# Expert weights stored in DRAM tile by tile, with one 4096-byte run a partition for each tile load

## The chip, the cores and the metric

One core of a Trainium2 chip runs the whole program. The metric is the device time in microseconds (us) of one execution. The engines are TensorE (PE; its weight loads are PEld), VectorE (DVE), ScalarE (ACT), GpSimd (POOL) and SyncE (SP), which here issues nearly all loads; 16 DMA engines move the bytes.

## The reference, cut to what matters

The program computes a one-layer hybrid block on 528 tokens, and then two layers of a second block on 512 latent tokens (and, in its first layer, 256 context tokens as well). Each of the two layers ends in a mixture of 16 experts, in which every expert takes its own best tokens:

```python
def ec_moe(h, w_router, w_gate, w_up, w_down):
    cap = EC_CAPACITY * n_tok // N_EXPERTS            # 64 of 512 tokens, 32 of 256
    aff = jax.nn.softmax(jnp.einsum('bnd,de->bne', h, w_router), axis=-1)
    g, idx = lax.top_k(jnp.swapaxes(aff, 1, 2), cap)
    xs = jax.vmap(lambda hb, ib: hb[ib])(h, idx)
    hid = jax.nn.silu(jnp.einsum('becd,edf->becf', xs, w_gate)) * jnp.einsum('becd,edf->becf', xs, w_up)
    ye = jnp.einsum('becf,efd->becd', hid, w_down) * g[..., None]
    return jax.vmap(lambda yb, ib: jnp.zeros((n_tok, d)).at[ib.reshape(-1)].add(yb.reshape(-1, d)))(ye, idx)
```

The model width and the experts' hidden width are both 1024, and all is float32. So `w_gate`, `w_up` and `w_down` hold 2 layers x 16 experts x 1024 x 1024 numbers each. Every weight is used once in an execution.

## The kernel before

`host_layout` arranges the inputs before the launch. The three expert tensors pass through it as they are. `body` traces the program; a planner orders the instructions of each engine, but inside `experts_both` the order of PE is that of the code.

In a layer the experts go two at a time, as eight pairs (`p_`, experts `ea` and `eb`). A pair needs its gate and up weights for each half `n` of the 1024 hidden columns, and then its down weights. All come as tiles of 256 rows by 512 columns, as `[128, 2, 512]`: 128 partitions, and in each of them two rows of 512 numbers (2048 bytes), which lie 128 rows apart in the matrix. A tile is 512 KB; a pair takes 32 tiles for gate and up and 16 for down, and a layer takes 384. `wtile` takes the next slot from a ring (`wslot`) and issues the load on SP's queue. A slot is free again when PE has used its old tile. The ring has NE + 6 + NX slots: 8 + 6 = 14 in layer 0 (`full`), 13 + 6 + 7 = 26 in layer 1. So the loads run ahead of PE by up to that many tiles.

In layer 0 `up_parts` and `down_parts` treat latent and context tokens together: `col4` (L139) runs four products side by side on strips of 32 columns of PE. In layer 1, the loop at L2235 to L2267, there are latent tokens alone, and `mm` (L136) runs two products side by side, on strips of 64 columns. In its first pairs the gathering of the chosen tokens (`next(more)`) is interleaved. After each pair `down_last` (L2036) scales the result and scatters it to the tokens. The last pair's results go through the final normalization (`last_norm`) to the output.

Of the kernel before, what the change touches and what calls it, by code (L numbers as in the profile page):

```python
# [26 lines left out]
def host_constants():  # L27

    p = np.arange(128)[:, None]
    c = np.arange(128)[None, :]  # L30
    parts = {}
    parts["ident"] = (p == c).astype(np.float32)
    sel = np.zeros((128, 8), np.float32)
    for i in range(3):
        sel[32 * i + np.arange(8), np.arange(8)] = -1.0
    parts["sel"] = sel
    parts["selm"] = ((p % 32 == c[:, :2]) & (p % 32 < 2)).astype(np.float32)
    parts["fbias"] = np.concatenate([np.zeros((128, 400)), np.where(c <= p, 0.0, NEG)], axis=1).astype(np.float32)
    t = (p % 64)
    parts["blk"] = ((p // 64) == (c // 64)).astype(np.float32)  # L40
    s = np.arange(64)[None, :]
    parts["low"] = (s <= t).astype(np.float32)
    parts["up"] = (t <= s).astype(np.float32)
    parts["sup"] = (t < s).astype(np.float32)
    for m in (1, 2, 4, 8, 16, 32):
        same = (t // (2 * m)) == (s // (2 * m))
        if m == 1:
            parts["lv1"] = (same & ((t // m) % 2 == 1) & ((s // m) % 2 == 0)).astype(np.float32)
        parts["lt%d" % m] = (same & ((s // m) % 2 == 1) & ((t // m) % 2 == 0)).astype(np.float32)
    parts["id64"] = (s == t).astype(np.float32)  # L50
    rs = np.ones((128, 576), np.float32)
    rs[:, ::64] = 0.0
    parts["reset"] = rs
    two = {}
    wlo = np.where(c >= p, 0.0, NEG)
    zero = np.zeros((128, 256))
    two["wb"] = np.concatenate([zero, wlo, zero[:, :128], np.where(c <= p, 0.0, NEG), zero], axis=1).astype(np.float32)
    two["flip"] = (((p // 64) == (c // 64)) & (p % 64 == 63 - c % 64)).astype(np.float32)
    tk = np.arange(SEQ)
    inv = (np.float32(10000.0) ** (-np.arange(16, dtype=np.float32) / np.float32(16))).astype(np.float32)  # L60
    d = np.arange(128) % 64
    pos = np.where((d < 32)[:, None], (tk // 64)[None, :], (tk % 64)[None, :]).astype(np.float32)
    ang = (pos * inv[d % 16][:, None]).astype(np.float32)
    two["cos"] = np.cos(ang).astype(np.float32)
    two["sin"] = (np.where(d % 32 < 16, -1.0, 1.0)[:, None] * np.sin(ang)).astype(np.float32)
    qc = (np.arange(128) % 64)[:, None]
    st = np.clip(qc - 8, 0, 48)
    kc = np.arange(64)[None, :]
    two["nmask"] = np.where((kc >= st) & (kc < st + 16), 0.0, NEG).astype(np.float32)
    two["mean"] = np.full((128, 128), 1.0 / 256, np.float32)  # L70
    two["iota1"] = np.tile(np.arange(1, 65, dtype=np.float32)[None, :], (128, 1))
    two["tokens"] = np.tile(np.arange(SEQ, dtype=np.float32)[None, :], (128, 1))

    def pack(parts):
        offs, cols, o = {}, [], 0
        for k, v in parts.items():
            offs[k] = (o, v.shape[1])
            cols.append(v)
            o += v.shape[1]
        return offs, np.ascontiguousarray(np.concatenate(cols, axis=1))  # L80
    return pack(parts) + pack(two)
# [10 lines left out]
def host_layout(given):  # L92

    g = dict(given)

    def cols(a, rows):
        return a.reshape(rows, 128).T
    v = [cols(g.pop(n), r) for n, r in VECTORS]
    v.append(g.pop("ffn_conv").reshape(3, 44, 128).transpose(2, 0, 1).reshape(128, 132))
    v.append(np.pad(g.pop("fox_f_bias").reshape(8, 1), ((0, 120), (0, 0))))  # L100
    v += [cols(g["norm_mix_post"], 8), cols(g["norm_ffn_pre"], 8),
          g["meta_tokens"][META - 2:].reshape(2, 8, 128).transpose(2, 1, 0).reshape(128, 16)]
    v += [cols(g.pop("c_2"), 8), cols(g.pop("c_ctx_2"), 8)]
    b = g.pop("b_mod_2")
    v += [cols(b[l], 48) for l in range(2)]
    c2 = [(g.pop(n), r) for n, r in CONV2]
    v += [cols(a[l], r) for l in range(2) for a, r in c2]
    g["vec"] = np.concatenate(v, axis=1)
    m = [np.concatenate([g.pop("rwkv_w_up")[0], g.pop("rwkv_a_up")[0]], axis=0), g.pop("rwkv_g_up")[0]]
    gates = [g.pop("lru_gate_a_w")[0], g.pop("lru_gate_x_w")[0]]  # L110
    for i in range(2):
        for w in gates:
            m.append(np.concatenate([np.pad(w[2 * i], ((0, 0), (0, 64))), np.pad(w[2 * i + 1], ((0, 0), (64, 0)))], axis=0))
    g["mats"] = np.concatenate(m, axis=1)
    g["nat_pad"] = np.pad(g.pop("nat_bias_2").reshape(-1), (64, 64))
    g["con"], g["con2"] = host_constants()[1::2]
    return g


# [7 lines left out]
def body(tc, A, out):  # L127
    nc = tc.nc
    ctx = ExitStack()
    PE, DV, AC, PL, SY = nc.tensor, nc.vector, nc.scalar, nc.gpsimd, nc.sync  # L130
# [28 lines left out]
    def nm(s):  # L159
        _n[0] += 1  # L160
        return "%s_%d" % (s, _n[0])
# [881 lines left out]
    for i in range(22):  # L1043
        res = []
        for hf in range(2):
# [5 lines left out]
            t = cv.tile([128, 512], F32, name=nm("cv"), tag="cv%d" % hf)  # L1051
# [98 lines left out]
    def layer(l):  # L1150
# [93 lines left out]
        for b in range(2):  # L1244
# [6 lines left out]
            n = 768 if full else 512  # L1251
# [3 lines left out]
            t = up_.tile([128, HW_], F32, name=nm("hx"), tag="hx%d" % b)  # L1255
# [229 lines left out]
        for i in range(4):  # L1485
# [4 lines left out]
            for j in range(4):  # L1490
# [3 lines left out]
                for h in range(2):  # L1494
                    ps = gps()
                    if j < 3:
                        c0, segs = 512 - w, [(512 - w, 128 * a0, w), (512, 512, 256)]
                    else:
                        c0, segs = 256, [(256, 512, 256), (512, 128 * a0, w)]
# [97 lines left out]
        for c in range(2 if full else 1):  # L1597
            t = rt.tile([128, 8, 16], F32, name=nm("wrm"), tag="wrm%d" % c)
# [5 lines left out]
            t = rt.tile([128, 16], F32, name=nm("brow"), tag="brow%d" % c)  # L1604
# [336 lines left out]
        def wslot(dt=F32):  # L1941
            i_ = ewn[0] % (NE + 6 + NX)
            ewn[0] += 1
            if i_ >= NE + 6:
                return ex.tile([128, 2, 512], dt, name=nm("ew"), tag="ew")
            if i_ < NE:
                return EW.tile([128, 2, 512], dt, name=nm("ew"), tag="ew")
            return WPw.tile([128, 2, 512], dt, name=nm("ew"), tag=("wr", "wh", "wl")[(i_ - NE) // 2], bufs=2)

        def wtile(name, e, k0, c0):  # L1950
            t = wslot()
            a = A[name]
            off = a.offset + ((l * 16 + e) * 1024 + 128 * k0) * 1024 + c0
            SY.dma_start(t, bass.AP(tensor=a.tensor, offset=off, ap=[[1024, 128], [128 * 1024, 2], [1, 512]]))
            return t

        if full:
# [78 lines left out]
        def down_last(p_, ea, eb, hT_):  # L2036
# [17 lines left out]
            for n, c in enumerate(HC):  # L2054
                for kh in range(4):
                    ws = [wtile("w_down_2", e, 2 * kh, 512 * n) for e in (ea, eb)]
                    for k in range(2):
                        K = 2 * kh + k
                        for po_, w_ in zip((0, 64), ws):
                            mm(psy[po_:po_ + 64, c], hT_[:, K, po_:po_ + 64], w_[:, k, :], K == 0, K == 7)  # L2060
                rows = norm_rows() if end and n else None
                t = outputs(psy, c, p_, t)
                if end and n:
                    g_ = gps()
                    for b in range(2):
                        hold(g_[:, HC[b]], 2 + b, 1)
                for b in range(4):
                    ps = held[b, n] if end else aps()
                    for i, y_ in enumerate(t[1:]):
                        mm(ps, oh_[:, 128 * b:128 * b + 128], y_, i == 0 and not end, i == 1)  # L2070
                    if not end:
                        DV.tensor_tensor(R_[b][:, c], R_[b][:, c], ps, ALU.add)
                if end:
                    skewed([last_norm(b, n, held[b, n], rows) for b in range(4)])
# [230 lines left out]
```

## Time and profile before

| | |
|---|---|
| median of 3 runs (lowest, highest) | 2784.72 us (2783.59, 2790.5) |
| the profiled execution, whole | 2780.72 us |
| its span, first to last instruction | 2778.9 us |
| PE busy in the span | 2578.3 us (93%) |
| moved by DMA | 578.65 MB, mean 208 GB/s |
| expert tile loads (3 tensors x 256 x 512 KB) | 768 |

The profiled execution is 4.0 us under the median of the runs, of which 1.8 us lie outside the span in any case. Layer 0's expert loads are issued from 1207 us on and its expert products run from 1305 to 1885 us; layer 1's run from 2258 to 2757 us. "DMA" in a row is the mean busy share of the 16 DMA engines. It is summed from the packets' own times, which overlap a little, so it can exceed 1.

### The profile page before, as it was taken

To read this page: it belongs to the slowest core of one execution; us is meant where nothing else is said; L and a number is where in the kernel's file an instruction comes from. 1 tells how busy PE (TensorE), PEld (TensorE's weight loads), DVE (VectorE), ACT (ScalarE), POOL (GpSimd) and SP (SyncE) were. 2 spreads that over 40 slices of the span, in tenths; PEclk is the share of its full clock that TensorE was granted. 3 is DMA by queue.
4 is the path that set the end of the run, shared out by engine and by line. 5 is a ranking of instruction groups with operands and counts; after the bars stand their busy time and mean duration, and the time that the engine had idled before them with its cause. 6 is when DMAs were issued, how large, how long until landed. Compare 5 with 4: busy or idle time off the path is not lost.

```text
span 2778.9 us, 46409 instructions
## 1 busy us (share of the span) xinstructions
PE 2578.3 (93%) x19286; PEld 1664.6 (60%) x19286; DVE 1217.6 (44%) x2252; ACT 898.5 (32%) x1617; POOL 161.4 (6%) x286
## 2 busy tenths in 40 slices
PE   7999999999998999996999999997999879999996
PEld 7877868999876877674333333324877744333322
DVE  4436555555656967565112121216868521121112
ACT  4344534343224357633211111116358421111001
POOL 0001000000000001013000000002001110000000
PEclk9999999999999999997999999997999979999999
DMA  4211144555762421424999999991430559999997
GB/s 141 61 36 42 36 160 137 180 162 173 237 210 81 96 49 49 140 91 155 333 386 345 381 345 380 347 340 43 104 77 18 199 203 387 386 386 386 387 387 275
DMA packets 378707, 578.65 MB, mean 208 GB/s; under 512 B 54384, under 2 KB 144880, under 8 KB 378240
## 3 DMA queue, kind: packets, MB, share of 16 engines
q1 hardware_dynamic: 354016, 550.82, 57.2%
q0 software_dynamic: 4928, 13.18, 1.9%
q10 hardware_dynamic: 19552, 11.68, 1.6%
q8 instruction: 152, 2.49, 0.4%
q14 instruction: 59, 0.48, 0.1%
HBM read 560.85 MB, written 5.24 MB: 204 GB/s over the span
## 4 chain that ended last, share of the span: by engine, by line
PE 65%; DVE 10%; DMA 10%; issue 4%; ACT 4%; POOL 2%; DVEq 0%; SPq 0%; ACTq 0%; POOLq 0%
PE g L136 26%; PE a L136 15%; PE g L139 11%; PE a L139 7%; DMA ew<-in_w_up_dram 6%; PE M L136 2%; DVE cy L1270 2%; DMA ew<-in_w_down_dram 2%; PE a L1409 2%; POOL rv L222 1%; DVE p L1382 1%; DMA wm<-in_w_mod_dram 1%; DVE wl L275 1%; DMA ln_g<-in_ln_g_dram 0%; DMA k<-k 0%
## 5 line engine op out<-in xcount | busy, mean ns | idle before, releaser
L136 PE MATMUL g<-ew,xsel 128*64 128x512 f32 x1024 | 262.7, 599 | 5.9 <-DMA ew<-in_w_up_dram 5.9
L139 PE MATMUL g<-ew,xsel 128*32 128x512 f32 x2048 | 254.1, 594 | 0.4 <-ACT xsel L1793 0.2
L275 DVE TENSOR_TENSOR wl<-wr,wh 128x1024 fp32r<-128x1024 f32 x95 | 115.2, 1213 | 187.9 <-ACT wh L274 179.5
L136 PEld LDWEIGHTS g<-ew,xsel 128*64 128x64 f32 x1024 | 75.9, 136 | 152.8 <-issue 113.8
L274 ACT ACTIVATE wh<-wr 128x1024 fp32r<-128x1024 f32 x95 | 99.6, 1049 | 189.1 <-PE g L136 121.1
L139 PEld LDWEIGHTS g<-ew,xsel 128*32 128x32 f32 x2048 | 68.3, 110 | 146.6 <-issue 136.0
L136 PE MATMUL g<-h2h,wh 128*128 128x256 f32 x704 | 144.1, 286 | 0.1
L136 PE MATMUL g<-h2h,wl 128*128 128x256 f32 x704 | 141.7, 283 | 0.0
L136 PE MATMUL g<-h2l,wh 128*128 128x256 f32 x704 | 141.3, 282 | 0.0
L139 PE MATMUL a<-ew,xsel 128*32 128x512 f32 x1024 | 140.0, 592 | 0.0
L136 PE MATMUL g<-ew,hT 128*64 128x512 f32 x512 | 131.2, 598 | 7.7 <-DVE y L2031 5.9
L139 PE MATMUL g<-ew,hT 128*32 128x512 f32 x1024 | 127.6, 605 | 4.0 <-DMA ew<-in_w_down_dram 4.0
L222 POOL TENSOR_TENSOR rv<-ru,epsc 128x1 f32<-128x1 f32 (+3 forms) x63 | 55.2, 880 | 1176.8 <-DVE ru L220 764.2
L2256 DVE TENSOR_TENSOR hid<-sg,g 128x512 f32<-128x512 f32 x16 | 11.0, 687 | 243.7 <-ACT sg L2255 219.5
L136 PEld LDWEIGHTS g<-h2h,wh 128*128 128x128 f32 x704 | 109.3, 190 | 10.5 <-ACT wh L274 7.4
L136 PEld LDWEIGHTS g<-h2h,wl 128*128 128x128 f32 x704 | 109.1, 190 | 0.0
L136 PEld LDWEIGHTS g<-h2l,wh 128*128 128x128 f32 x704 | 108.5, 189 | 0.4 <-issue 0.4
L1389 ACT ACTIVATE p<-p,mx 128x768 f32<-128x768 f32 (+4 forms) x120 | 91.6, 764 | 42.2 <-DVE mx L1382 39.9
L1270 DVE SCALAR_TENSOR_TENSOR cy<-hx,cvc,cy 128x798 f32<-128x798 f32 (+1 forms) x120 | 103.5, 898 | 1.8
L2148 DVE TENSOR_TENSOR hid<-sg,g 128x512 f32<-128x512 f32 x16 | 11.0, 688 | 207.9 <-ACT sg L2147 207.9
L136 PEld LDWEIGHTS g<-ew,hT 128*64 128x64 f32 x512 | 38.3, 136 | 88.2 <-issue 60.3
L1370 ACT ACTIVATE pT<-a 128x512 f32<-128x512 f32 (+1 forms) x152 | 78.2, 538 | 35.6 <-PE a L1409 33.0
(660 smaller groups left out, 5329.8 us busy)
## 6 DMA issues: line engine op xcount, KB each, us to landing
ew<-in_w_gate_dram SPq DMA_DIRECT2D x256, 512.0 KB, 10.8
ew<-in_w_up_dram SPq DMA_DIRECT2D x256, 512.0 KB, 10.5
ew<-in_w_down_dram SPq DMA_DIRECT2D x256, 512.0 KB, 10.8
wm<-in_w_mod_dram SPq DMA_DIRECT2D x96, 512.0 KB, 4.8
wr<-in_ffn_up_dram SPq DMA_DIRECT2D x44, 512.0 KB, 5.1
wr<-in_w_in_dram SPq DMA_DIRECT2D x42, 512.0 KB, 4.1
wr<-in_ffn_down_dram SPq DMA_DIRECT2D x22, 512.0 KB, 5.1
wr<-in_w_out_dram SPq DMA_DIRECT2D x16, 512.0 KB, 3.8
```

Source lines behind the costliest of these rows:

```text
L136: return PE.matmul(o, l, r, start=start, stop=stop, skip_group_check=True)
L139: PE.matmul(o, l, r, start=start, stop=stop, skip_group_check=True, tile_position=(0, o.start_partition()))
L222: PL.tensor_tensor(v[:P], u[:P], epsc[:P, :w], ALU.pow)
L274: AC.activation(hi, raw, AF.Copy)
L275: DV.tensor_tensor(lo, raw, f(hi), ALU.subtract)
L1270: DV.scalar_tensor_tensor(cy[b], hx[b][:, i:i + N], cvw[l][:, 2 * i + b:2 * i + b + 1], cy[b], ALU.mult, ALU.add)
L1370: AC.activation(dst, src, AF.Copy)
L1382: DV.tensor_tensor_reduce(t[:, n:n + w], v, b, -1.0, m, ALU.add, ALU.min, m2)
L1389: AC.activation(t[:, :e], t[:, :e], AF.Exp, scale=-1.0, bias=m, accum_out=sm)
L1409: PE.transpose(ps[:, 128 * i:128 * i + 128], t[:, 128 * i:128 * i + 128], ident)
L2148: DV.tensor_tensor(hid[:, 512 * n:512 * n + 512], sg, psx[:, 512:1024], ALU.mult)
L2256: DV.tensor_tensor(hid[:, 512 * n:512 * n + 512], sg, psx[:, 512:1024], ALU.mult)
```

## The change

The host now permutes each expert tensor to [layer, expert, block of 256 rows, half of the columns, partition, row of two, 512]. A tile of `wtile` is then one contiguous 512 KB piece of DRAM, in which each partition's two rows stand one behind the other: 4096 bytes a partition. The tile in SBUF, the slots, the queue, the number of loads and all arithmetic are as before.

```diff
     g["con"], g["con2"] = host_constants()[1::2]
+    for n in ("w_gate_2", "w_up_2", "w_down_2"):
+
+        g[n] = g[n].reshape(2, 16, 4, 2, 128, 2, 512).transpose(0, 1, 2, 5, 4, 3, 6)
     return g
...
         def wtile(name, e, k0, c0):
             t = wslot()
-            a = A[name]
-            off = a.offset + ((l * 16 + e) * 1024 + 128 * k0) * 1024 + c0
-            SY.dma_start(t, bass.AP(tensor=a.tensor, offset=off, ap=[[1024, 128], [128 * 1024, 2], [1, 512]]))
+            SY.dma_start(t, A[name][l, e, k0 // 2, c0 // 512])
             return t
```

## Rows read from the trace of the kernel before

**Rows 1.** The page's 40 equal slices of the span (69.5 us each).
```profile
PE   7999999999998999996999999997999879999996
DMA  4211144555762421424999999991430559999997
GB/s 141 61 36 42 36 160 137 180 162 173 237 210 81 96 49 49 140 91 155 333 386 345 381 345 380 347 340 43 104 77 18 199 203 387 386 386 386 387 387 275
```

**Rows 2.** Stretches in layer 1's experts: length, busy time (instructions), PEclk, DMA share, GB/s.
```profile
2260.00:2270.00 10.00, 10.00 (x62) 5.54 (x60) 0.00 (x0) 2.09 (x4) 0.00 (x0) 1.00 0.79 268
2270.00:2280.00 10.00, 10.00 (x56) 4.49 (x54) 0.00 (x0) 2.37 (x4) 0.00 (x0) 1.00 1.00 363
2280.00:2290.00 10.00, 10.00 (x54) 4.35 (x52) 0.69 (x1) 1.93 (x4) 0.00 (x0) 1.00 1.02 363
2300.00:2735.00 435.00, 409.75 (x1742) 153.90 (x1741) 68.76 (x117) 40.51 (x71) 0.00 (x0) 1.00 1.05 386
```

**Rows 3.** The chain that ended last, layer 1's experts: start, us, what.
```profile
2403.82 14.73 PE g L136 x66
...
2463.53 14.73 PE g L136 x66
...
2720.95 11.17 DMA ew<-in_w_up_dram
...
2732.16 2.80 PE g L136 x10
```

**Rows 4.** Waits of PE from 2253 to 2510 us: total us, times, longest.
```profile
PE a L1814 <- DVE tk L1811: 14.4, 1, 14.4
```

**Rows 5.** Waits of PE from 2510 to 2757 us.
```profile
PE g L136 <- DMA ew<-in_w_up_dram: 5.9, 19, 0.8
```

**Rows 6.** SP's loads as layer 1's experts begin: start, us, what.
```profile
2219.74 2.34 SPq L1954 DMA_DIRECT2D ew<-in_w_gate_dram  x2
2260.98 0.88 SPq L1954 DMA_DIRECT2D ew<-in_w_up_dram  x2
```

**Rows 7.** Stretches in layer 0's experts, columns as in rows 2.
```profile
1700.00:1750.00 50.00, 49.75 (x468) 15.83 (x464) 4.80 (x7) 4.63 (x8) 0.00 (x0) 1.00 1.05 386
1333.00:1885.00 552.00, 542.75 (x4777) 186.37 (x4769) 96.88 (x141) 69.54 (x115) 0.00 (x0) 0.99 0.98 359
```

**Rows 8.** Waits of PE from 1333 to 1885 us: the longest.
```profile
PE g L139 <- DMA ew<-in_w_down_dram: 4.0, 1, 4.0
```

**Rows 9.** The chain that ended last, at that wait.
```profile
1872.38 4.77 DMA ew<-in_w_down_dram
```

**Rows 10.** DMA from 2350 to 2700 us: packets, then SP's queue as share of 16 engines.
```profile
DMA packets 70076, 135.28 MB, mean 387 GB/s; under 512 B 4123, under 2 KB 4123, under 8 KB 70060
...
q1 hardware_dynamic: 70060, 135.06, 104.5%
```

**Rows 11.** DMA over the whole span: packets, the two instruction queues.
```profile
DMA packets 378707, 578.65 MB, mean 208 GB/s; under 512 B 54384, under 2 KB 144880, under 8 KB 378240
...
q8 instruction: 152, 2.49, 0.4%
q14 instruction: 59, 0.48, 0.1%
```

**Rows 12.** DMA issues over the span: count, KB each, median us to landing.
```profile
ew<-in_w_up_dram SPq DMA_DIRECT2D x256, 512.0 KB, 10.5
...
con<-in_con_dram SPq DMA_DIRECT2D x2, 1056.0 KB, 7.2
x<-in_x_dram SPq DMA_DIRECT2D x4, 512.0 KB, 7.3
```

**Rows 13.** DMA packets from 8 to 10 us, 752 to 754 us and 1116 to 1120 us.
```profile
DMA packets 237, 0.85 MB, mean 424 GB/s; under 512 B 26, under 2 KB 31, under 8 KB 237
...
DMA packets 230, 0.82 MB, mean 411 GB/s; under 512 B 23, under 2 KB 23, under 8 KB 230
...
DMA packets 425, 1.55 MB, mean 387 GB/s; under 512 B 47, under 2 KB 47, under 8 KB 425
```

## The prediction

> **What bounds the kernel now.** I read the slices of the span first [rows 1]. PE is busy nearly everywhere, so its busy time says little; what sets the expert stages apart is the DMA row. There are two stretches at 9, one in each layer's experts, and in layer 1 it stands flat at 386 or 387 GB/s. A flat rate under changing work suggests a limit of the transfers themselves, so I looked at each stage for who waits for whom.
>
> Layer 1 first. From 2300 to 2735 us the DMA engines move 386 GB/s at a share of 1.05 [rows 2]. A tile of 524,288 bytes at 386.5 GB/s (135.28 MB in 350 us [rows 10]) costs 1.357 us. PE alone is faster: while its work is the bound, one pair takes 59.7 us (2463.53 less 2403.82, the same piece of two successive pairs [rows 3]), and 59.7 / 48 tiles is 1.244 us a tile. So each pair falls 5.4 us behind its own consumption, and the 26 slots that were filled beforehand pay for it. One sees them pay: up to 2510 us PE's waits name no DMA at all, and the longest, 14.4 us, is for the choosing of tokens, ahead of the products [rows 4]; after it, PE waits for up tiles, 19 times [rows 5]. At the end the chain hangs on a load that lands at 2732.1 us, and PE goes on from there [rows 3]. That landing is set by the DMA rate since the ring was last full, not by PE.
>
> Layer 0 is the other case. There the four products side by side keep PE at 468 instructions in 50 us, with 49.75 us busy [rows 7], and the stage takes 552 us for 384 tiles, 1.44 us a tile: slower than a transfer (1.357). In the whole stage PE waits for a load once, 4.0 us [rows 8], and that is a load issued late, when its slot came free at 1872.38; its 4.77 us are mostly the latency of a load with few others beside it [rows 9]. The DMA row of 386 there is prefetching, not a bound.
>
> **The change, part by part.** *The permutation* is done before the launch and moves no instruction on the chip: nothing. *SP's issue:* still 768 loads, waits and slots alike; SP is paced by slots and landings, about 8 loads in flight (10.5 us to landing [rows 12] over 1.357). Nothing either way, and if one issue cost 0.1 us more it would still be hidden in the 1.28 us between them. *PE, DVE, ACT:* the same tile at the same place, nothing.
>
> *The packets.* Today a tile is 256 packets of 2048 bytes: the saturated stretch has 70,060 packets on SP's queue for 135.06 MB, with 4,123 small ones [rows 10]. After it, if a packet is one contiguous run, it is 128 of 4096 bytes. That a packet may be that long the trace shows: 467 packets are not under 8 KB, which are the 152 and 59 of the instruction queues [rows 11] and 256 for two loads with 8,448 bytes a partition [rows 12]. So 768 x 128 = 98,304 packets go away.
>
> What a 4096-byte packet costs must come from loads of that row length. There are three short stretches where large packets average about 4.1 KB (bytes over packets not under 2 KB): 424 GB/s at 8 to 10 us, 411 at 752 to 754, 387 at 1116 to 1120 [rows 13]. The first is the load of `x`, whose tile is laid out just as an expert tile will be, 128 rows of 4096 bytes one behind the other [rows 12]; the others are modulation weights at a wider pitch, the last with small transfers ahead. Both ends stay in: 387 (nothing gained) and 424. I take 410, the middle row and near their mean (407): 1.279 us a tile, 0.078 less than now. Two microseconds are a short look, hence the wide bounds.
>
> Weighed against that: the Trainium skill (DMA: Bandwidth & Descriptors, Why small descriptors are slow) gives a packet about 3 cycles beside one for each 32 bytes. By it a 4096-byte packet would gain only 134 / 131, 2.3%, and a tile would cost about 1.326 us, by my estimate. By row a tile saves 0.078 us, by rule 0.030. The row decides, and the rule's time is a rival below.
>
> *The sum in layer 1.* 26 tiles are issued by 2222 us and the next at 2260.98 [rows 6]. From 2260 to 2290 the ring is still full and PE's freeing of slots holds the loads back: 268, 363, 363 GB/s [rows 2], 9.94 MB, 19 tiles; I leave that as it is. The last up tile is number 7 x 48 + 32 = 368, so 323 tiles remain at the DMA's own rate. Check: 323 x 1.357 = 438 us from 2290 gives 2728, beside 2732.1 seen. After: 323 x 1.279 = 413, a gain of 25.1 us. PE's 1.244 stays under 1.279, so DMA stays the bound, but now by only 1.7 us a pair: the slots stay nearly full for longer and hold a load back now and then. I take off 1 us. From the last up tile to the end it is PE's down products and the final normalization, 46.8 us to the span's end, as before: the 16 down tiles behind it come sooner too, within 16 x 1.279 = 20.5 us instead of 21.7.
>
> *The sum in layer 0.* PE is the cover: nothing, and at most 4.0 us if that one late load came earlier. It waits for a slot, so I take 0.5.
>
> Together 24.6 us: 2780.7 less 24.6 is 2756.1 for an execution like the profiled one. The runs' median before is 4.0 us higher, so I forecast 2760 for the median after.
>
> **Rivals.**
>
> *A smaller cost per packet.* If weights stream as the two stretches of modulation weights do and not as `x` does, the rate is their mean, 399 GB/s [rows 13]: 1.314 us a tile, 323 x 0.043 = 13.9 us, about 2771. For it: these are weights, and two rows of three. Against it: the 387 begins behind small transfers, and the layout is that of `x`. The Trainium skill's rule above would end further on this side, at 323 x 0.030 = 9.7 us, 2775.
>
> *More than assumed.* At 424 GB/s a tile costs 1.237 us, less than PE's 1.244; then PE's pair is the bound while tokens are gathered, and the gain stops near 323 x 0.113 = 36 us, 2748. For it: `x`, the same layout, at 424. Against it: a two-microsecond stretch may count packets begun before it.
>
> *No change.* The run is not merged: the tile still has two halves a partition, and a load cut along them stays at 256 packets. Or 2048 bytes are already at the rate that the memory gives. Then 2785. For it: the tile's shape is unchanged, no load in this trace shows such a merge, and 387 occurs with long rows as well. Against it: 411 and 424. The Trainium skill (DMA: Bandwidth & Descriptors, Specifications) puts the line rate at 512 bytes and up, by which nothing would be gained; the saturated 386.5 under rows of 411 and 424 doesn't bear it out.
>
> *Slower.* A tile is now one piece of 512 KB, and 16 engines read inside it in step; if that crowds part of the memory, the rate falls. It decides at 386.5 GB/s. At 348 (10% less) a tile costs 1.507 us: layer 1 loses 323 x 0.15 = 48 us, and layer 0, whose PE needs a tile each 1.44 us, becomes bound by loads and loses 384 x 0.07 = 27 us, so about 2860. For it: the pattern is new for the weights. Against it: `x` has it, and streams fastest of all.
>
> **How the numbers follow.** A measurement here tells about 0.3% (8.4 us) from no change. My case, 400 to 418 GB/s, 2752 to 2770: 0.66. More: 0.07. A smaller packet cost, 2770 to 2776: 0.12. No change: 0.10. Slower: 0.05. Hence faster 0.85, same 0.10, slower 0.05. The range 2745 to 2776 holds the first three but for a little at the low end, and leaves the last two out.
>
> **What the profile after would show.** Packets on SP's queue lower by 98,304; expert loads landing some 0.6 us sooner under load (8 x 0.078); DMA at 400 to 418 GB/s in layer 1's flat stretch; PE's first waits for up tiles tens of microseconds after 2510; layer 0's stage within 2 us of 552. Wrong would be: the packets unchanged (not merged), the packets halved at 387 GB/s (the run length was not the limit), or the rate up and the landing of the last up tile not earlier (slots, or PE, bind layer 1).

## The result and the profile after

The changed kernel takes 2758.03 us (median of 4 runs, 2752.61 to 2761.47), the kernel before, measured beside it, 2785.55 us (2783.59 to 2790.50). The ratio is 0.9897, with a 95% interval of 0.9876 to 0.9918: faster by about 27 us. The forecast was 2760, in a range of 2745 to 2776. The profiled execution took 2758.13 us with a span of 2756.4, so 22.6 us less than the profiled execution before.

In the line numbers of the changed kernel, the products are three lines further (L136 and L139 of before are L139 and L142), and what stands behind `wtile` is one further.

The page's slices and its DMA totals, after (to be laid beside [rows 1, 11]):

```profile
PE   7999999999998989996999999997899969999996
DMA  4211153555672321433798999992342349999997
GB/s 143 59 36 33 39 168 117 183 162 183 209 243 83 84 57 30 143 109 138 298 394 350 374 359 366 367 357 71 90 81 50 131 165 399 407 409 409 409 409 282
DMA packets 280403, 578.65 MB, mean 210 GB/s; under 512 B 54384, under 2 KB 144880, under 8 KB 279936
```

The flat stretch at the end has gone from 386 or 387 to 409 GB/s. There are 378,707 less 280,403 = 98,304 packets fewer for the same 578.65 MB, which is 768 tiles x 128: each pair of 2048-byte runs has become one packet. The numbers under 512 B and under 2 KB are those of before.

The flat stretch alone, after, packets and SP's queue. It is 2350 to 2650 us, 300 us, where [rows 10] has 350; the rates can be compared, the counts can't:

```profile
DMA packets 33621, 122.57 MB, mean 409 GB/s; under 512 B 3735, under 2 KB 3735, under 8 KB 33606
...
q1 hardware_dynamic: 33606, 122.37, 102.3%
```

Stretches of layer 1 and of layer 0, after (answers to [rows 2, 7]): length, busy time and instructions of PE, PEld, DVE, ACT and POOL, then PEclk, DMA share, GB/s.

```profile
2260.00:2270.00 10.00, 10.00 (x54) 4.74 (x54) 0.00 (x0) 1.69 (x3) 0.00 (x0) 1.00 0.61 210
2270.00:2280.00 10.00, 10.00 (x59) 5.35 (x59) 0.00 (x0) 2.26 (x4) 0.00 (x0) 1.00 0.99 370
2280.00:2290.00 10.00, 10.00 (x54) 4.26 (x50) 0.69 (x1) 2.44 (x3) 0.00 (x0) 1.00 1.02 390
2300.00:2700.00 400.00, 381.96 (x1712) 149.56 (x1710) 68.79 (x117) 41.79 (x73) 0.00 (x0) 1.00 1.03 408
1333.00:1885.00 552.00, 543.68 (x4801) 183.87 (x4802) 98.32 (x142) 72.93 (x119) 0.00 (x0) 0.99 0.93 359
```

Below I call the time from the first to the last expert product of a layer its *stage*. The view by tile gives both ends. Layer 1's two kinds of products on expert tiles, before, with the starts of the first and the last:

```profile
L136 PE MATMUL g<-ew,xsel x1024: 592/592/644, 2258.2 to 2734.4; 128*64 128x512 f32 x171
L136 PE MATMUL g<-ew,hT x512: 592/592/644, 2301.4 to 2756.2; 128*64 128x512 f32 x171
```

and after:

```profile
L139 PE MATMUL g<-ew,xsel x1024: 592/592/644, 2260.1 to 2711.8; 128*64 128x512 f32 x171
L139 PE MATMUL g<-ew,hT x512: 592/592/644, 2303.4 to 2733.6; 128*64 128x512 f32 x171
```

Layer 1's stage went from 498.0 (2756.2 less 2258.2) to 473.5 us: 24.5 us saved. Layer 0's, read in the same way, went from 578.8 to 576.5. From the last product to the span's end it is 22.7 us before and 22.8 after. Layer 1 began 1.9 us later than before, although layer 0 was 2.3 us shorter: what lies ahead of the expert stages moves by some microseconds between executions. 24.5 less 1.9 is the 22.6 of the profiled executions, to a tenth.

The chain that ended last shows the same change of hands. Its shares by line from 2510 to 2757 us, before:

```profile
by line: DMA ew<-in_w_up_dram 52.7%; PE g L136 23.6%; DMA ew<-in_w_down_dram 13.1%; PE a L136 7.2%; DVE y L2031 1.8%; issue 0.7%; DVE hid L2256 0.3%; PE a L2265 0.3%; ACT y L2032 0.3%; ACT sg L2255 0.2%; SPq L1954 0.1%; ACTq L2032 0.0%
```

After, the whole chain from 2400 us on (start, us, what), where one piece recurs in each pair of experts:

```profile
2405.74 14.73 PE g L139 x66
...
2465.43 14.73 PE g L139 x66
...
2526.28 14.73 PE g L139 x66
...
2586.00 14.73 PE g L139 x66
...
2640.73 14.73 PE g L139 x66
```

Before, two thirds of that chain are loads. After, no load of an expert tile stands in it from 2400 us on: the piece recurs each 59.7 to 60.9 us, and the last two of these are 54.7 us apart, since no gathering of tokens is left.

PE's waits from 2510 to 2740 us, after (answers to [rows 5]; total us, times, longest):

```profile
PE a L139 <- ACT y L2033: 4.7, 3, 1.6
PE g L139 <- DVE y L2032: 4.2, 5, 0.9
PE a L2266 <- DVE hid L2257: 3.6, 5, 1.4
```

Neither these nor the smaller rows left out name a load. Yet before, the waits of PE's products for loads came to only 7.4 us (5.9 for up tiles [rows 5] and 1.5 for down tiles), and 24.5 were saved. The rest was hidden in PE's busy time. The groups of products from 2510 us to the end (busy us, mean ns | idle before), before:

```profile
L136 PE MATMUL g<-ew,xsel 128*64 128x512 f32 x491 | 131.7, 600 | 5.9 <-DMA ew<-in_w_up_dram 5.9
L136 PE MATMUL g<-ew,hT 128*64 128x512 f32 x256 | 68.3, 601 | 4.9 <-DVE y L2031 3.4 <-DMA ew<-in_w_down_dram 1.5
```

and after:

```profile
L139 PE MATMUL g<-ew,xsel 128*64 128x512 f32 x492 | 117.9, 596 | 0.0
L139 PE MATMUL g<-ew,hT 128*64 128x512 f32 x256 | 64.0, 596 | 3.4 <-DVE y L2032 3.4
```

The products overlap each other (491 of 600 ns in 131.7 us). The group is "busy" for 13.8 + 4.3 us longer before: the same products overlap less. With the 7.4 us of waits that makes 25.5, about what the stage saved. What held the products apart stands in the rows of the weight loads (PEld), which go ahead of the products. Their waits for expert tiles from 2510 to 2740 us (total us, times, longest), before:

```profile
PEld g L136 <- DMA ew<-in_w_up_dram: 24.3, 22, 1.7
PEld g L136 <- DMA ew<-in_w_down_dram: 13.1, 18, 1.2
PEld g L136 <- DMA ew<-in_w_gate_dram: 6.7, 9, 0.8
```

and after:

```profile
PEld g L139 <- DMA ew<-in_w_up_dram: 2.4, 6, 0.9
PEld g L139 <- DMA ew<-in_w_gate_dram: 2.1, 6, 0.6
PEld g L139 <- DMA ew<-in_w_down_dram: 0.7, 3, 0.3
```

That is 44.1 us before and 5.2 after. These waits lie partly under products that still run, so they are more than what the stage saved.

### The profile page after: what moved, and what is told of

Its sections match the earlier page's. It is cut to its first block, busy times and chain, and to the rows that moved or that the text cites. A ratio compares the mean times of both kernels' runs of the same rounds, so it can differ in the third digit from the quotient of the medians.

```text
span 2756.4 us, 46409 instructions
## 1 busy us (share of the span) xinstructions
PE 2564.9 (93%) x19286; PEld 1662.6 (60%) x19286; DVE 1216.9 (44%) x2252; ACT 899.6 (33%) x1617; POOL 162.0 (6%) x286
## 2 busy tenths in 40 slices
DMA packets 280403, 578.65 MB, mean 210 GB/s; under 512 B 54384, under 2 KB 144880, under 8 KB 279936
## 4 chain that ended last, share of the span: by engine, by line
PE 71%; DVE 11%; issue 4%; ACT 4%; DMA 3%; POOL 2%; SPq 0%; DVEq 0%; ACTq 0%; POOLq 0%
PE g L139 30%; PE a L139 15%; PE g L142 12%; PE a L142 7%; PE M L139 2%; DVE cy L1273 2%; PE a L1412 2%; POOL rv L225 1%; DVE p L1385 1%; DMA wm<-in_w_mod_dram 1%; DVE wl L278 1%; DMA ln_g<-in_ln_g_dram 0%; DMA k<-k 0%; DMA wr<-in_w_out_dram 0%; DVE y L2032 0%
## 5 line engine op out<-in xcount | busy, mean ns | idle before, releaser
L139 PE MATMUL g<-ew,xsel 128*64 128x512 f32 x1024 | 248.5, 596 | 0.0
L142 PE MATMUL g<-ew,xsel 128*32 128x512 f32 x2048 | 248.1, 596 | 0.4 <-ACT xsel L1796 0.2
L139 PEld LDWEIGHTS g<-ew,xsel 128*64 128x64 f32 x1024 | 74.0, 137 | 134.8 <-issue 121.9
L142 PEld LDWEIGHTS g<-ew,xsel 128*32 128x32 f32 x2048 | 65.1, 110 | 147.7 <-issue 142.2
L139 PE MATMUL g<-h2h,wh 128*128 128x256 f32 x704 | 144.1, 286 | 0.1
L139 PE MATMUL g<-h2h,wl 128*128 128x256 f32 x704 | 141.4, 282 | 0.0
L139 PE MATMUL g<-h2l,wh 128*128 128x256 f32 x704 | 141.3, 282 | 0.0
L142 PE MATMUL a<-ew,xsel 128*32 128x512 f32 x1024 | 133.0, 592 | 0.0
L139 PE MATMUL g<-ew,hT 128*64 128x512 f32 x512 | 127.0, 596 | 6.2 <-DVE y L2032 5.9
L142 PE MATMUL g<-ew,hT 128*32 128x512 f32 x1024 | 127.4, 606 | 3.0 <-DMA ew<-in_w_down_dram 3.0
L139 PEld LDWEIGHTS g<-h2h,wh 128*128 128x128 f32 x704 | 109.2, 190 | 10.5 <-ACT wh L277 7.4
L139 PEld LDWEIGHTS g<-h2h,wl 128*128 128x128 f32 x704 | 109.0, 189 | 0.0
L139 PEld LDWEIGHTS g<-h2l,wh 128*128 128x128 f32 x704 | 108.5, 189 | 0.4 <-issue 0.4
L139 PEld LDWEIGHTS g<-ew,hT 128*64 128x64 f32 x512 | 38.1, 137 | 84.2 <-issue 70.6
```

The costliest lines, as they stand in the source:

```text
L139: return PE.matmul(o, l, r, start=start, stop=stop, skip_group_check=True)
L142: PE.matmul(o, l, r, start=start, stop=stop, skip_group_check=True, tile_position=(0, o.start_partition()))
```

## The experiments

Each ran beside the kernel before on the same chip; ratios are against that. The theories of the first four: **A**, the length of a run in DRAM sets the rate; **B**, its place does (one 512 KB piece for a tile, or not).

**contig_2k** keeps each tile in one contiguous piece, but with the partition's two rows 256 KB apart in it, so runs stay at 2048 bytes:

```diff
-        g[n] = g[n].reshape(2, 16, 4, 2, 128, 2, 512).transpose(0, 1, 2, 5, 4, 3, 6)
+        g[n] = g[n].reshape(2, 16, 4, 2, 128, 2, 512).transpose(0, 1, 2, 5, 3, 4, 6)
...
-            SY.dma_start(t, A[name][l, e, k0 // 2, c0 // 512])
+            SY.dma_start(t, A[name][l, e, k0 // 2, c0 // 512].rearrange("k p c -> p k c"))
```

> Each tile is one contiguous 512 KB piece of DRAM, as in the change, but a partition's two rows lie 256 KB apart in it, so that the runs stay at 2048 bytes. Theory A (the length of the run, by a fixed time in each packet, sets the rate): as the kernel before, 386 GB/s in layer 1's flat stretch, 354,016 packets on SP's queue, about 2785 us, ratio 1.000. Theory B (the place sets it: a tile in one piece instead of two pieces 512 KB apart): as the changed kernel, about 409 GB/s and 2758 us, ratio 0.990.

Measured: 2781.93 us, ratio 0.9993 (0.9981 to 1.0005); layer 1's stage 497.5. DMA from 2350 to 2700 us:

```profile
DMA packets 70073, 135.27 MB, mean 386 GB/s; under 512 B 4123, under 2 KB 4123, under 8 KB 70057
```

Packets and rate are those of before [rows 10]. A contiguous tile alone is worth nothing and costs nothing: B falls.

**run4k_pitch8k** has runs of 4096 bytes, but 8192 apart, with the two tiles of a row block interleaved:

```diff
-        g[n] = g[n].reshape(2, 16, 4, 2, 128, 2, 512).transpose(0, 1, 2, 5, 4, 3, 6)
+        g[n] = g[n].reshape(2, 16, 4, 2, 128, 2, 512).transpose(0, 1, 2, 4, 5, 3, 6)
...
-            SY.dma_start(t, A[name][l, e, k0 // 2, c0 // 512])
+            SY.dma_start(t, A[name][l, e, k0 // 2, :, c0 // 512])
```

> Runs of 4096 bytes a partition, but 8 KB apart, so that a tile is spread over 1 MB and another tile lies between its runs. Theory A (length of the run): as the changed kernel, 255,712 packets, 409 GB/s, about 2758 us, ratio 0.990. Theory B (tile in one piece): the rate falls back towards 386 GB/s, 2770 to 2785 us.

Measured: 2768.76 us, ratio 0.9925 (0.9898 to 0.9951); 280,403 packets. In the profiled execution layer 1's stage was 479.1 us. The rate from 2350 to 2700 us:

```profile
GB/s 408 405 392 395 411 397 405 411 409 408 409 410 408 409 410 410 407 410 410 407 409 410 408 407 405 409 408 392 406 408 375 395 396 410 409 408 412 409 407 411
```

The run length brings most of the gain without the contiguous tile, but A's 2758 is missed by 11 us. The rate has dips to 375 that the changed kernel hardly has (390 at the lowest in the same stretch), and the stage is 5.6 us longer. The rest of the difference to the changed kernel lies ahead of layer 1, which began 5.7 us later in the profiled execution. Whether the dips are the pitch's doing stays open.

**contig_1k** goes the other way: four runs of 1024 bytes for each partition, in a contiguous tile.

```diff
-        g[n] = g[n].reshape(2, 16, 4, 2, 128, 2, 512).transpose(0, 1, 2, 5, 4, 3, 6)
+        g[n] = g[n].reshape(2, 16, 4, 2, 128, 2, 2, 256).transpose(0, 1, 2, 5, 3, 6, 4, 7).reshape(2, 16, 4, 2, 4, 128, 256)
...
-            SY.dma_start(t, A[name][l, e, k0 // 2, c0 // 512])
+            SY.dma_start(t.rearrange("p k (h c) -> p (k h) c", h=2),
+                         A[name][l, e, k0 // 2, c0 // 512].rearrange("q p c -> p q c"))
```

> A tile is one contiguous piece, but in runs of 1024 bytes (four a partition). Theory A: 2048 bytes take 84.8 ns on an engine at 386.5 GB/s and 4096 bytes 160.2 ns at 409, so a packet has 9.4 ns of its own and 75.4 ns for 2048 bytes; 1024 bytes then take 47.1 ns, 348 GB/s, 1.507 us a tile. Layer 1 loses 323 x 0.15 = 48 us against the kernel before, and layer 0, whose PE takes 1.44 us a tile, becomes bound by loads and loses 384 x 0.07 = 27 us: about 2860 us, ratio 1.027. Theory B: a tile in one piece stays at 400 GB/s or more, 2758 us.

Measured: 2872.39 us, ratio 1.0308 (1.0288 to 1.0327). DMA from 2350 to 2700 us:

```profile
DMA packets 122478, 121.83 MB, mean 348 GB/s; under 512 B 3706, under 2 KB 122463, under 8 KB 122463
```

Layer 1's stage grew by 50.7 us, layer 0's by 35.6: there too the loads are the bound now, and PE waits for them 44 times, 21.2 us in all, where it waited once before. With both the mechanism of the prediction's first part is shown from the other side: layer 1 pays for each change of the rate that was tried, layer 0 in full only below some point between 386 and 348.

**stream** is loads alone, on SP's queue, 24 of 1 MB for each pattern, through 12 buffers; no part of the block is computed, and the output is a copy of weights. The patterns in order: runs of 2048, 512, 1024, 2048, 4096 and 8192 bytes in a contiguous piece, then 2048-byte runs in the pattern of before (4 KB apart, a partition's rows 512 KB apart), then 4096 again.

> Loads alone, without any of the computation: the output is a copy of weights. Eight stretches of 24 loads of 1 MB each (128 partitions of 8 KB), in runs of 2 KB, 512 B, 1 KB, 2 KB, 4 KB and 8 KB that follow one another in DRAM, then 2 KB runs 4 KB apart with 512 KB between a partition's runs (the pattern of the kernel before), then 4 KB once more. Theory A, from 9.4 ns a packet and 36.8 ns a KB: 512 B 295 GB/s, 1 KB 348, 2 KB 386, 4 KB 409, 8 KB 422; the pattern of the kernel before as 2 KB, 386. Theory B: the 2 KB runs that follow one another are at 400 or more, and the pattern of the kernel before alone is at 386.

Its slices (13.7 us each) and packets:

```profile
GB/s 317 387 387 387 382 290 290 290 290 290 290 332 348 348 348 348 366 387 387 387 387 404 410 409 410 415 422 422 422 423 386 387 387 387 391 410 410 409 409 280
DMA packets 92738, 203.45 MB, mean 371 GB/s; under 512 B 3136, under 2 KB 27712, under 8 KB 89664
```

Run lengths of 512 B, 1, 2, 4 and 8 KB stream at 290, 348, 387, 410 and 422 GB/s, and the pattern of before at the 387 of a contiguous piece. Divided over 16 engines, a packet takes 28.2, 47.1, 84.7, 160 and 311 ns, which is 37.65 ns for each KB of 1024 bytes (the 36.8 that was expected is for 1000) and 9.4 ns for the packet, whatever its length. Between 512 bytes and 8 KB this line misses none of the five by 1%.

**layer1_only** and **layer0_only** use the new layout in one layer, and the old in the other. The host stacks one layer of each, and `wtile` chooses the access by `l` (in layer0_only the test is `l == 0`):

```diff
+            if l == 1:
+                off = l * 16777216 + (((e * 4 + k0 // 2) * 2) + c0 // 512) * 131072
+                ap = [[1024, 128], [512, 2], [1, 512]]
+            else:
+                off, ap = ((l * 16 + e) * 1024 + 128 * k0) * 1024 + c0, [[1024, 128], [128 * 1024, 2], [1, 512]]
+            SY.dma_start(t, bass.AP(tensor=a.tensor, offset=a.offset + off, ap=ap))
```

> The new order of the weights in layer 1's half of the three tensors alone; layer 0 loads as before. By the prediction the whole gain lies in layer 1: ratio 0.990, as the whole change, 2758 us. Rival: layer 0's rate counts too (its DMA row was at 386 for long stretches), and a part of the gain is lost: ratio 0.993 to 0.997.

> The new order in layer 0's half alone. By the prediction PE is the bound there: at most 0.5 to 1 us less than the kernel before, ratio 1.000. Rival: 0.995 to 0.997.

Measured: 2756.35 us, ratio 0.9911 (0.9883 to 0.9939), and 2779.79, ratio 0.9992 (0.9977 to 1.0008). Layer 1's stage is 474.4 and 499.5 us, layer 0's 576.6 and 574.7. Nearly all of the gain is layer 1's; what layer 0 gains is too little for the runs to show (the interval of layer0_only reaches from 6 us less to 2 us more).

The pattern written here has the partition's two rows as a dimension of their own. Layer1_only has 329,555 packets all the same, 49,152 fewer than before, which is 384 tiles x 128: the runs were merged because they follow one another in DRAM and in the partition, however the pattern is written.

**new_no_up_loads** and **old_no_up_loads** ask how much of layer 1's time the loads still cost: its up tiles are not loaded, and the gate tile is used in their place, so a third of the bytes is gone and the products stay. Theory **C**: behind the change PE's own work is the bound; **D**: the loads still are.

```diff
-                    ga, gb, ua, ub = [wtile(w, e, 2 * kh, 512 * n) for w in ("w_gate_2", "w_up_2") for e in (ea, eb)]
+                    ga, gb = [wtile("w_gate_2", e, 2 * kh, 512 * n) for e in (ea, eb)]
+                    ua, ub = ga, gb
```

> The changed kernel without the loads of layer 1's up weights (128 of its 384 tiles): the gate tile is multiplied twice, so PE, ACT and DVE do the same work, on other numbers. Theory C (after the change PE and not the loads sets layer 1's end): within 3 us of the changed kernel, 2755 to 2758 us, ratio 0.989 to 0.990. Theory D (the loads still set it, as the prediction had it): with a third of them gone it drops by the rest of the lag, 6 us a late pair and more, to about 2740 or below, ratio 0.984.

> The same left out of the kernel before (layer 1's up loads; the gate tile is multiplied twice). This is the time when layer 1 never waits for a load. Theory C: the same as the changed kernel without these loads, 2755 to 2758 us, so that the change already took all that faster loads can give in layer 1. Theory D: the same as the changed kernel without them too, but at about 2740.

Measured: 2713.76 us, ratio 0.9753 (0.9729 to 0.9778), with the new layout, and 2712.61, ratio 0.9735 (0.9710 to 0.9760), with the old. That the two agree shows that the layout is worth nothing where loads don't bind. But 45 us under the changed kernel is what neither theory gave, and the chain says why it is no measure of the loads. Pieces of it, new_no_up_loads:

```profile
2297.40 8.73 PE g L139 x38
...
2350.32 8.73 PE g L139 x38
...
2404.10 8.73 PE g L139 x38
```

A pair takes 53 us there, while tokens are still gathered, not 59.7. With fewer loads the planner puts PE's work in another and denser order: products in long runs, where the changed kernel has single pairs of them between pieces of the gathering. So two things were changed at once.

**new_code_order, old_code_order, code_order_half_up** hold PE's order fixed: the loop over layer 1's pairs stands in a block in which PE's instructions keep the order of the code. The third also loads just the first of the two row blocks of each up tile, and uses it twice; that is a sixth of layer 1's bytes, with PE's work and order unchanged.

```diff
-        for p_ in () if full else range(8):
+        with ExitStack() if full else tc.manual_schedule(engines={mybir.EngineType.PE}):
+            for p_ in () if full else range(8):
...
-            SY.dma_start(t, A[name][l, e, k0 // 2, c0 // 512])
+            if name == "w_up_2" and not full:
+                SY.dma_start(t[:, 0], A[name][l, e, k0 // 2, c0 // 512, :, 0])
+            else:
+                SY.dma_start(t, A[name][l, e, k0 // 2, c0 // 512])
...
-                                mm(psx[po_:po_ + 64, c0:c0 + 512], xx[:, K, :], w_[:, k, :], *fl)
+                                mm(psx[po_:po_ + 64, c0:c0 + 512], xx[:, K, :], w_[:, 0 if c0 else k, :], *fl)
```

> The changed kernel, but in layer 1's experts PE works in the order of the code (gate and up products of a pair, its transposes, its down products) in place of the planner's order. This order is the same in the two kernels beside it. Theory C (PE alone sets the end after the change): the time moves with what the order costs PE, up or down by more than 5 us. Theory D (the 409 GB/s set it, PE is close behind): the loads end when they ended, so 2753 to 2760 us, unless the order costs PE more than the lag of 2 to 6 us a pair.

> The kernel before with PE in the order of the code in layer 1's experts. Its loads run at 386 GB/s and set layer 1's end, whatever the order: 2780 to 2787 us, ratio 0.998 to 1.001, by both theories.

> As the changed kernel with PE in the order of the code, and of each up tile of layer 1 only the first of a partition's two rows is loaded (it is multiplied twice): a sixth of layer 1's bytes is left out, PE's order and work stay. Theory C (PE sets the end): within 3 us of the run with whole tiles. Theory D (loads set it): a pair's loads fall from 61.5 to 51.3 us and PE's pace of 53 to 56 us takes over, 30 to 45 us less, 2715 to 2725 us.

| | whole, us | ratio (interval) | layer 1's stage |
|---|---|---|---|
| old_code_order | 2787.96 | 1.0016 (1.0000 to 1.0032) | 503.7 |
| new_code_order | 2760.50 | 0.9929 (0.9907 to 0.9952) | 479.6 |
| code_order_half_up | 2752.88 | 0.9897 (0.9874 to 0.9919) | 469.6 |

PE's waits from 2300 us to the end, in new_code_order:

```profile
PE a L139 <- ACT y L2033: 23.6, 15, 1.6
PE g L139 <- DMA ew<-in_w_up_dram: 3.5, 15, 0.8
PE a L139 <- DVE y L2034: 3.4, 15, 0.2
```

and the first two in code_order_half_up:

```profile
PE a L139 <- ACT y L2036: 23.6, 15, 1.6
PE a L139 <- DVE y L2037: 3.4, 15, 0.2
```

Here old_code_order came out 1 us above its range and new_code_order at the upper end of D's. In this order the layout saves 24.1 us of the stage, as in the planner's, and what the loads still cost is 10.0 (479.6 less 469.6). That is more than C's 3 and less than D's 30 to 45: neither had the size. After the change the loads and PE's own order bind within some 10 us of each other.

**rows_late** takes up layer 0's one wait, on the changed kernel: the normalization (`rows = norm_rows()`) is put behind the last pair's down products instead of ahead of them.

```diff
-                rows = norm_rows()
                 down_parts(7)
+                rows = norm_rows()
```

> The changed kernel, with the two rows of the final normalization of layer 0 loaded after the last pair's down tiles instead of ahead of them. They take two slots of the ring, which holds the last two down tiles back. Expected: PE's one wait for a load in layer 0 (3.0 us, and 3 to 4 us at half clock behind it) goes away, and layer 0's expert products end 3 to 6 us sooner; in all 2752 to 2756 us. Rival: the wait is taken over by another late load and nothing changes, 2758 us.

Measured: 2753.21 us, ratio 0.9901 (0.9870 to 0.9931). Around the wait, the changed kernel (columns as above):

```profile
1871.00:1876.00 5.00, 4.65 (x44) 1.08 (x36) 2.00 (x2) 2.11 (x2) 0.00 (x0) 1.00 0.41 80
1876.00:1883.00 7.00, 4.34 (x20) 1.55 (x24) 0.45 (x1) 0.00 (x0) 0.00 (x0) 0.63 0.94 292
```

and rows_late:

```profile
1871.00:1876.00 5.00, 5.00 (x52) 1.32 (x44) 0.00 (x0) 0.00 (x0) 0.00 (x0) 1.00 1.02 320
1876.00:1883.00 7.00, 6.29 (x55) 1.80 (x47) 3.65 (x4) 3.64 (x5) 0.00 (x0) 1.00 0.35 99
```

PE's products wait for no expert tile in layer 0 any more, and its stage is 569.7 us, 6.8 less than the changed kernel's. That is the upper end: four other profiled executions with the new layout in layer 0 (layer0_only, new_no_up_loads, new_code_order, code_order_half_up) have 572.8 to 574.7, so the gain is 3 to 7 us. The whole is 4.8 us under the changed kernel's median; it is the fastest of the versions with the full work, but the intervals of the two overlap, so that the gain stands in the stage and not yet in the runs.

## Why the prediction was right

**The packets.** A packet is one contiguous run: 98,304 fewer, to the packet.

**The rate.** I took 410 GB/s from three short rows [rows 13]; it is 409 in the kernel, and 410 in the stream of 4096-byte runs. The two ends of the bound turn out to be no properties of the run length: 387 at 1116 us began behind small transfers, and the 424 of `x` was a two-microsecond look, which no steady stream of 4096-byte runs reached. That the middle row was the right one was luck in part.

**Layer 1.** Forecast 24.1 us (25.1 less 1), measured 24.5, 23.6 in layer1_only and 24.1 in code order. **Layer 0.** Forecast 0.5, measured 2.3 in the profiled execution and nothing that can be told from zero in layer0_only's runs. Laid side by side, the profiled executions say about 3: the stage takes 576.4 to 578.9 us in the five with 2048-byte runs there (before, contig_2k, layer1_only, old_no_up_loads, old_code_order; mean 577.5) and 572.8 to 576.5 in the five with 4096 (mean 574.1). PE remains the cover there, but not wholly. I had read the waits of its products alone, one of 4.0 us [rows 8]; it is 3.0 after, still for the slot that comes late. The weight loads waited too, from 1300 to 1930 us, before and then after:

```profile
PEld g L139 <- DMA ew<-in_w_up_dram: 5.0, 9, 1.0
PEld g L142 <- DMA ew<-in_w_up_dram: 1.6, 2, 1.0
```

**The tail, SP, PE, DVE, ACT:** unchanged, as said; the instructions stand in the same order on each engine.

**The sum.** 24.6 forecast; the profiled executions differ by 22.6, the medians by 27.5, the interval of the ratio is 23 to 35 us. Some 24 us of layer 1 and 3 of layer 0 make about the 27.5.

**What was off.** The step that failed is "DMA stays the bound", with waits for up tiles "tens of microseconds after 2510": after the change PE's products wait for no load in layer 1, and the chain holds none. The per-tile prices were right (409 GB/s makes a tile 1.282 us and a pair's 48 tiles 61.5), and the rate stays flat at 409, so transfers do run without a pause. What I did not work out is the stock. Rates alone don't say which of two ends last when one has a start of 26 slots. By the prediction's own prices the loads fall 323 x 0.035 = 11 us back, 9 tiles. By the pieces of the chain the lag is about 1.8 us in each of five pairs (59.7 us) and 6.8 in two (54.7), so PE gains about 23 us on the loads in the stage, 18 tiles, by my estimate. The ring holds 26, of which about eight are under way there (10.2 us from issue to landing, over 1.282). So the stock is just not used up, and loads and PE end together. The last pair of up loads, start and us of its issue, before and after:

```profile
2719.30 2.01 SPq L1954 DMA_DIRECT2D ew<-in_w_up_dram  x2
2697.22 1.91 SPq L1955 DMA_DIRECT2D ew<-in_w_up_dram  x2
```

Counted from the stage's first product, that is 24.0 us sooner: the sum for the loads (24.1) was right. That the time followed it, although PE and not the loads set the end, is because PE's own pace ended within a few microseconds of them. The prediction did not know this, so that part was luck. It also means that the 36 us of the rival *More than assumed* were not to be had in this order of PE: its products wait for no load any more, and its weight loads for 5.2 us after 2510.

The 0.6 us by which loads were to land sooner under load came true. The median from issue to landing, 2350 to 2700 us, before and after:

```profile
ew<-in_w_up_dram SPq DMA_DIRECT2D x88, 512.0 KB, 10.8
ew<-in_w_up_dram SPq DMA_DIRECT2D x96, 512.0 KB, 10.2
```

Over the whole span up tiles land 3.1 us sooner (7.4 for the 10.5 of [rows 12]). That is layer 0, from 1333 to 1885 us, where the slots hold the loads back:

```profile
ew<-in_w_up_dram SPq DMA_DIRECT2D x122, 512.0 KB, 9.3
ew<-in_w_up_dram SPq DMA_DIRECT2D x122, 512.0 KB, 6.9
```

The mean rate there is 359 GB/s in both, so with shorter landings fewer loads are under way at a time.

**The rivals.** *A smaller cost per packet* (399 GB/s, 2771) falls: the kernel's rate rose by 5.8% (409 over 386.5), the stream's by 5.9%. The Trainium skill's rule (DMA: Bandwidth & Descriptors, Why small descriptors are slow) of about 3 cycles a packet beside one for each 32 bytes gave 2.3%. The runs disagree with it: 37.65 ns a KB is 1.18 ns for 32 bytes, and the packet's own 9.4 ns are 8 of those, not 3. *More than assumed* falls: 4096-byte runs do not sustain 424. The Trainium skill (DMA: Bandwidth & Descriptors, iDMA fabric) gives a stream of 4 KiB rows alone 408.7 GB/s, and the 409 and 410 here agree. *No change* falls, with its two grounds: the run was merged, and 2048 bytes are not at the limit. That 512 bytes suffice for the line rate, as the Trainium skill (DMA: Bandwidth & Descriptors, Specifications) has it, is contradicted by 290 GB/s beside 422. *Slower*, by crowding in one piece, falls with contig_2k at 386 GB/s; but its price was tried by another way to the same rate: at 348 GB/s I had put 2860, and contig_1k took 2872, its layer 1 50.7 us longer (48 forecast) and its layer 0 35.6 (27).

Not tried: runs of 8192 bytes in the kernel (they need tiles of 1 MB, other slots), and the denser order of PE with all loads in place.

## What to carry to other kernels

Where the DMA row stands flat at the same rate under changing work, look at the packets' lengths: between 2 KB and 4 KB runs there are 6% of the rate, and a layout in DRAM that makes a partition's rows contiguous takes them with nothing changed in the program but the loads' access pattern. What it is worth is read in the stage where the chain runs through loads; where PE needs longer for a tile than its transfer, it is worth little (about 3 us in layer 0 here). Don't size such a stage's gain by the waits of the products: 7.4 us of them stood here for 24.5, and the rest was in products that overlapped less while they were "busy". The waits of the weight loads (44.1 us) were the sign of it. And to say what bounds the stage after a change, compare the lag that builds up over the stage with the stock of tiles in the ring, and not the two rates alone.

## What the runs showed of the hardware that was not expected

- The rate of 512 KB or 1 MB loads followed from the run length, but for run4k_pitch8k's dips, at 37.65 ns a KB and 9.4 ns a packet for each of 16 engines: 290, 348, 387, 410, 422 GB/s from 512 B to 8 KB. For runs of 2 KB it made no difference whether a partition's runs lay 256 KB or 512 KB apart (387 both in stream).
- A small wait in layer 0 cost more than its length in some executions. PE stands without work for 3.0 us in the changed kernel, and behind that the granted clock is 0.63 on average from 1876 to 1883 us (0.53 in the same stretch before the change): for most of it the lower level, 1.2 of 2.4 GHz. Where the wait is gone the clock stays at 1.00, and the stage is 6.8 us shorter. The fall does not always follow: behind the same wait of 2.8 us in code_order_half_up and of 3.3 us in run4k_pitch8k the clock stays at 1.00 to the end of the stage, and the stage takes 573.7 and 573.4 us. So of the 6.8 us about 4 go with the wait and about 3 with the clock, by these single executions; why it fell in one and not in the other stays open.
- With no wait for a load in either, layer 1's stage took 430 us in the order that the planner found for fewer loads and 470 in code order: more than the layout is worth. Beside the order itself, the code order's 27.0 us of waits for ACT and DVE, its granted clock of 0.97 (1.00 in the other, to 2650 us) and the loads that each leaves out differ; no run separates them. Two products of a strip pair alone between small pieces show as 1.00 us in the chain, 32 products (16 pairs) in a stream as 7.02 us, 0.44 a pair.
